# One chunk of a recurrent mixer: two matmuls moved up beside two others, and one start flag for a PSUM tile instead of three

## The chip, the cores and the metric

The kernel runs on one core of a Trainium2 chip. The metric is the device time of one execution in microseconds; several executions are given by their median. A core has five engines with a queue of instructions each: TensorE (PE, with its weight loads shown apart as PEld), VectorE (DVE), ScalarE (ACT), GpSimd (POOL) and SyncE (SP, which issues DMAs here). Engines wait for each other by semaphores only. Matmuls write PSUM; ScalarE and VectorE copy from there to SBUF.

## The reference

One decoder layer on a sequence of 2048 tokens of width 1024: an RMS norm, one input projection, two groups of heads side by side (sliding-window attention, and RWKV-7 time mixing), an output projection, a gated MLP with a short convolution, and a last norm. The change lies in the time mixing. For each of its 8 heads (64 wide) a state S of 64 x 64 is carried along the sequence:

```
def step(S, inp):
    r_t, w_t, k_t, v_t, a_t, b_t = inp
    sa = jnp.einsum('bhvk,bhk->bhv', S, a_t)
    S = S * w_t[:, :, None, :] + sa[..., None] * b_t[:, :, None, :] \
        + v_t[..., None] * k_t[:, :, None, :]
    return S, jnp.einsum('bhvk,bhk->bhv', S, r_t)
```

## The kernel before, in words

The time mixing is done in chunks of 64 tokens. The sequence has 4 blocks of 512 tokens, the 8 heads are 4 pairs, and 16 times (4 blocks x 4 pairs, here called head pairs) a chain of 8 chunks is run by `chain`, in order: 128 chunks in all. Two heads of a pair lie on partitions 0 to 63 and 64 to 127, so each product of a chunk is two instructions, one for each half (`hs`).

A chunk works on one PSUM tile `pc` with three columns of 64 and has these steps:

- W (line 896): the products with the incoming state SV, into `pc[:, 0]`, with 128 rows of the array and 64 columns for each head. ScalarE copies them to Pt.
- y1: the first half of the output, W (its other columns) with SV, into another PSUM tile, `pY`.
- TT (line 909): the inverted triangle with Pt, into `pc[:, 1]`, with 64 rows and 64 columns. ScalarE copies it to Ut.
- IK (line 913): the identity and the keys with SV, into `pc[:, 2]`: the carried state and the part of the values. It has 128 rows and 64 columns, and it does not need Ut.
- Bt (line 914): the part that comes by Ut, added in `pc[:, 2]`, with 64 rows and 64 columns. ScalarE scales the sum into the next chunk's SV.
- XB: the second half of the output, with Ut, into `pY`, with 64 rows and 64 columns.

The first `start=True` that reaches a PSUM bank clears the marks by which a later matmul knows whether to add or to overwrite.

The order of all engines in this part is written out: every matmul, activation and vector operation goes through a helper that ties it behind the one before on its engine (`in_order`; matmuls are recorded as line 104, activations as 110, vector operations as 124, GpSimd's as 132, DMAs as 170). Between the steps of a chunk `fill` places other work: the next pair's input projections (`pin_...`), its preparation, the attention, the output of the pair before. How much goes into each gap is set by tables of assumed costs, which the change leaves alone. Only DMAs and some GpSimd work are ordered by a scheduler.

For the pair that comes next one triangle per chunk has to be inverted: `px` (TensorE), `XB` (VectorE), a DMA to `dL` and back as `LL`, a substitution of 31 steps on VectorE (`Mt` and `M`, woven between its other work), a DMA to `dT` and back as `TT`, a transpose `T` on VectorE, and two small rounds of matmuls `ph`. All of it stands inside the current pair's chain.

Of the kernel before, what the change touches and what calls it, by code (L numbers as in the profile page):

```python
# [83 lines left out]
def hybrid_trunk_kernel(  # L84
# [9 lines left out]
    def in_order(key, i):  # L94
        if order["on"]:
            last = order.get(key)
            if last is not None:
                tc.add_manual_dep(i.ins, last.name,
                                  mybir.DependencyInfo(mybir.DependencyClass.NoSync, mybir.DependencyReason.DATA),
                                  reason="issue order")  # L100
            order[key] = i.ins

    def mm(**kw):
        in_order("pe", nc.tensor.matmul(**kw))  # L104
# [4 lines left out]
    def act(*args, **kw):  # L109
        in_order("act", nc.scalar.activation(*args, **kw))  # L110
# [86 lines left out]
    with ExitStack() as A:  # L197
# [20 lines left out]
        def fin512(name):  # L218
            return tp.tile([P, BLK], F32, tag="f", name=name, bufs=2)
# [76 lines left out]
        hs = [slice(0, 64), slice(64, 128)]  # L296
# [101 lines left out]
        def defer(us, fn, key=None):  # L398
            clk["n"] += 1
            todo.append((clk["t"] + us, clk["n"], fn, key))  # L400
            todo.sort(key=lambda d: d[:2])
# [6 lines left out]
        def need(key):  # L408
            while any(d[3] == key for d in todo):
                todo.pop(0)[2]()  # L410
# [213 lines left out]
        def v3(ap):  # L624
            return ap.rearrange("p (c t) -> p c t", t=C)
# [257 lines left out]
        def chain(n, fill):  # L883
            b, j = divmod(n, NPAIR)
            u = f"{b}_{j}"
            S = U[n]
            W, SV, XB, Bt, IK, TT, E = S["W"], S["SV"], S["XB"], S["Bt"], S["IK"], S["TT"], S["E"]
            St = state[j]
            pY = None
            for c in range(NCH):  # L890
                pc = ps_ch.tile([P, 3, C], F32, tag="ch", name=f"pc_{u}_{c}")
                Pt = tp.tile([P, C], F32, tag="Pt", name=f"Pt_{u}_{c}")
                Ut = tp.tile([P, C], F32, tag="Ut", name=f"Ut_{u}_{c}")
                eC = E[:, c, C:C + 1]
                for hh, s in enumerate(hs):
                    mm(out=pc[s, 0], lhsT=W[:, c, hh, 0:C], rhs=SV[:, c, hh, :], start=True, stop=True)
                act(Pt, pc[:, 0], AF.Copy)
                def y1(c=c, pY=pY):
                    for hh, s in enumerate(hs):
                        mm(out=pY[s, c], lhsT=W[:, c, hh, C:2 * C], rhs=SV[:, c, hh, :], start=True, stop=False)  # L900
                if c > 0:
                    y1()
                fill()
                if c == 0:
                    need("ycopy")
                    pY = ps_ch.tile([P, NCH, C], F32, tag="cy", name=f"pY_{u}")
                    y1(pY=pY)
                for hh, s in enumerate(hs):
                    mm(out=pc[s, 1], lhsT=TT[s, c, :], rhs=Pt[s], start=True, stop=True)
                act(Ut, pc[:, 1], AF.Copy)  # L910
                fill()
                for hh, s in enumerate(hs):
                    mm(out=pc[s, 2], lhsT=IK[:, c, hh, :], rhs=SV[:, c, hh, :], start=True, stop=False)
                    mm(out=pc[s, 2], lhsT=Bt[s, c, :], rhs=Ut[s], start=False, stop=True)
                if c < NCH - 1:
                    for hh, s in enumerate(hs):
                        act(SV[s, c + 1, hh, :], pc[s, 2], AF.Copy, scale=eC[s])
                else:
                    act(St, pc[:, 2], AF.Copy, scale=eC)
                for hh, s in enumerate(hs):  # L920
                    mm(out=pY[s, c], lhsT=XB[s, c, C:2 * C], rhs=Ut[s], start=False, stop=True)
                fill()
            Y = S["Y"] = tp.tile([P, NCH, C], F32, tag="Y", name=f"Y_{u}")
            ysq = fin512(f"ysq_{u}")

            def go0():
                act(Y, pY, AF.Copy)
                act(ysq, pY.rearrange("p c v -> p (c v)"), AF.Square, scale=0.125)
                defer(Q["y1"], go1, f"y_{u}")
            var = tp.tile([P, 8], F32, tag="var", name=f"var_{u}")  # L930

            def go1():
                vred(out=var, in_=v3(ysq), axis=AX.X, op=ALU.add)
                gts(out=var, in0=var, scalar1=LNX_EPS, scalar2=None, op0=ALU.add)
                gtt(out=var, in0=var, in1=mhalf, op=ALU.pow)
                defer(Q["y2"], go2, f"y_{u}")

            def go2():
                gtt(out=Y, in0=Y, in1=var.unsqueeze(2).broadcast_to([P, NCH, C]), op=ALU.mult)
            defer(0.1, go0, "ycopy")  # L940
# [155 lines left out]
        for n in range(-2, NU + 1):  # L1096
# [120 lines left out]
            def fill():  # L1217
                st["hop"] += 1
                was = st["done"]
                tick(Q["hop"])  # L1220
                run_until(MS + (1 - MS) * st["hop"] / hops)
                while dense and st["done"] - was < MINQ:
                    c, fn = dense.pop(0)
                    tick(c)
                    fn()
                    st["done"] += c
# [3 lines left out]
            if 0 <= n < NU:  # L1230
                chain(n, fill)
# [601 lines left out]
```

## Time and profile before

| what | value |
|---|---|
| time, median of 3 runs | 2750.26 us (2749.35 to 2753.12) |
| the profiled execution's own time | 2754.07 us |
| its span, first to last instruction | 2752.3 us |
| TensorE busy in the span | 2640.4 us, 96% |
| VectorE, ScalarE, GpSimd busy | 62%, 47%, 53% |
| mean granted clock of TensorE | 0.977 of 2.4 GHz |
| stage of the chunk chains | 126 to 1270 us |

The profile is of one execution. Durations below are in microseconds unless marked ns. A row of the order of time gives start, duration, engine, line, operation, what is written and read, and in brackets the engine's idle time before it and what ended it. An fp32 matmul instruction shows as two records. Ends of matmuls are modelled, so it is starts that are compared.

### The profile page before, as it was taken

How to read it: one execution, taken by the hardware profiler on the slowest of the kernel's cores; microseconds unless marked ns; L12 is line 12 of the kernel's file. 1: busy time of each engine (PE TensorE's matmuls, PEld its weight loads, DVE VectorE, ACT ScalarE, POOL GpSimd, SP SyncE). 2: the span in 40 equal slices, each digit the busy share in tenths (PEclk: the TensorE clock that was granted, in tenths of full speed). 3: DMA queues.
4: the chain of work that ended last, by engine and by line, in shares of the span. 5: the costliest groups of instructions: out<-in, count | busy, mean ns of one | idle time of the engine just before them, and what ended most of it. 6: DMA issues, size and time to landing. Idle time of an engine off the chain costs nothing.

```text
span 2752.3 us, 42156 instructions
## 1 busy us (share of the span) xinstructions
PE 2640.4 (96%) x15211; PEld 2051.3 (75%) x15211; DVE 1713.7 (62%) x3217; ACT 1288.9 (47%) x2737; POOL 1460.6 (53%) x1356
## 2 busy tenths in 40 slices
PE   7799999999999999998989999999999999999997
PEld 5566777777777767676867878788788888878885
DVE  6567666676667556743666677677766765453334
ACT  4356655656556545543434344336333343343343
POOL 6333443344343333422346777777666665484594
PEclk9899999999999999999999999999999999999998
DMA  4222222222223222234663444446333336743354
GB/s 128 63 61 71 70 72 69 67 55 72 64 72 95 56 61 64 75 101 135 199 213 104 151 132 142 139 164 199 107 104 111 102 98 229 245 141 100 107 173 149
DMA packets 333108, 313.94 MB, mean 114 GB/s; under 512 B 102576, under 2 KB 254274, under 8 KB 332898
## 3 DMA queue, kind: packets, MB, share of 16 engines
q1 hardware_dynamic: 332290, 310.71, 36.9%
q8 instruction: 119, 1.95, 0.3%
q14 instruction: 91, 0.75, 0.1%
q10 hardware_dynamic: 608, 0.53, 0.1%
HBM read 229.26 MB, written 81.92 MB: 113 GB/s over the span
## 4 chain that ended last, share of the span: by engine, by line
PE 74%; DVE 9%; DMA 6%; POOL 4%; issue 3%; ACT 3%; SPq 0%; POOLq 0%; ACTq 0%; DVEq 0%
PE d L104 14%; PE q_g L104 12%; PE q_u L104 12%; PE pc L104 6%; PE pin_r L104 3%; PE pin_k L104 3%; PE poa L104 3%; PE pin_q L104 3%; DVE M L124 2%; PE px L104 2%; DVE Mt L124 2%; PE pS L104 2%; PE po L104 2%; PE pO L104 1%; PE pin_v L104 1%
## 5 line engine op out<-in xcount | busy, mean ns | idle before, releaser
L1255 POOL TENSOR_TENSOR ul_a<-sa,uh_a 128x512 fp32r<-128x512 f32 x154 | 208.8, 1362 | 154.7 <-ACT uh_a L110 151.3
L1255 POOL TENSOR_TENSOR ul_u<-s_u,uh_u 128x512 fp32r<-128x512 f32 x154 | 215.7, 1410 | 137.6 <-ACT uh_u L110 131.2
L1255 POOL TENSOR_TENSOR ul_g<-s_g,uh_g 128x512 fp32r<-128x512 f32 x154 | 221.7, 1448 | 55.4 <-ACT uh_g L110 51.3
L104 PE MATMUL q_g<-h2h,uh_g 128*128 128x512 f32 x616 | 242.2, 393 | 7.8 <-DVE u_g L1470 6.3
L104 PE MATMUL q_u<-h2h,uh_u 128*128 128x512 f32 x616 | 240.2, 390 | 2.2 <-DVE ct L1470 1.5
L104 PE MATMUL q_g<-h2h,ul_g 128*128 128x512 f32 x616 | 240.7, 391 | 0.4 <-POOL ul_g L1255 0.4
L104 PE MATMUL q_g<-h2l,uh_g 128*128 128x512 f32 x616 | 241.0, 391 | 0.0
L104 PE MATMUL q_u<-h2h,ul_u 128*128 128x512 f32 x616 | 239.9, 390 | 1.0 <-POOL ul_u L1255 1.0
L104 PE MATMUL q_u<-h2l,uh_u 128*128 128x512 f32 x616 | 239.7, 389 | 0.0
L104 PE MATMUL d<-ul_b,uh_a 128*128 128x512 f32 x616 | 232.3, 391 | 6.7 <-DVE ul_b L1467 6.7
L104 PE MATMUL d<-uh_b,ul_a 128*128 128x512 f32 x616 | 227.7, 391 | 3.5 <-POOL ul_a L1255 3.5
L110 ACT ACTIVATE uh_a<-sa 128x512 fp32r<-128x512 f32 x154 | 97.3, 632 | 233.4 <-PE d L104 126.1
L104 PE MATMUL d<-uh_b,uh_a 128*128 128x512 f32 x616 | 204.1, 389 | 0.0
L110 ACT ACTIVATE uh_u<-s_u 128x512 fp32r<-128x512 f32 x154 | 94.9, 628 | 220.9 <-DVE s_u L1467 116.6
L1467 DVE TENSOR_TENSOR ul_b<-wd,uh_b 128x512 fp32r<-128x512 f32 x55 | 68.2, 1240 | 189.3 <-ACT uh_b L110 184.0
L110 ACT ACTIVATE uh_g<-s_g 128x512 fp32r<-128x512 f32 x154 | 95.1, 629 | 183.2 <-PE q_u L104 101.7
L124 DVE TENSOR_TENSOR Mt<-M,LL 128x60 f32<-128x60 f32 (+24 forms) x496 | 153.2, 309 | 35.7 <-DMA LL<-dL 27.2
L124 DVE TENSOR_TENSOR M<-M,Mt 128x60 f32<-128x60 f32 (+24 forms) x496 | 163.0, 329 | 10.9
L124 DVE SCALAR_TENSOR_TENSOR cc<-g,fcst,cc 128x1024 f32<-128x1024 f32 x88 | 145.7, 1674 | 29.1 <-ACT cc L110 28.4
L104 PEld LDWEIGHTS q_g<-h2h,uh_g 128*128 128x128 f32 x616 | 116.6, 189 | 34.7 <-DVE u_g L1470 8.0
L104 PEld LDWEIGHTS d<-ul_b,uh_a 128*128 128x128 f32 x616 | 116.3, 189 | 31.3 <-DVE ul_b L1467 7.1
L104 PEld LDWEIGHTS d<-uh_b,ul_a 128*128 128x128 f32 x616 | 115.8, 189 | 29.4 <-POOL ul_a L1255 5.6
(370 smaller groups left out, 7141.3 us busy)
## 6 DMA issues: line engine op xcount, KB each, us to landing
sa<-actc SPq DMA_DIRECT2D x77, 512.0 KB
s_g<-in_ffn_w_gate_dram SPq DMA_DIRECT2D x44, 512.0 KB
s_u<-in_ffn_w_up_dram SPq DMA_DIRECT2D x44, 512.0 KB
actc<-cc SPq DMA_DIRECT2D x88, 256.0 KB
actc<-sa SPq DMA_DIRECT2D x66, 256.0 KB
wd<-in_ffn_w_down_dram SPq DMA_DIRECT2D x22, 512.0 KB
s_cat<-catT SPq DMA_DIRECT2D x20, 512.0 KB
x<-in_x_dram SPq DMA_DIRECT2D x16, 512.0 KB
```

What stands on the lines that cost most here:

```text
L104: in_order("pe", nc.tensor.matmul(**kw))
L110: in_order("act", nc.scalar.activation(*args, **kw))
L124: in_order("dve", f(*args, **kw))
L1255: nc.gpsimd.tensor_tensor(out=out, in0=in0, in1=in1, op=ALU.subtract)
L1467: nc.vector.tensor_tensor(out=out, in0=in0, in1=in1, op=ALU.subtract)
```

## The change

The IK products are issued right behind the W products. Their `start=True`, and that of the TT products, become `start=False`: the W products' `start=True` clears the marks for all three columns of `pc`, and each column's first write overwrites.

```
                 for hh, s in enumerate(hs):
                     mm(out=pc[s, 0], lhsT=W[:, c, hh, 0:C], rhs=SV[:, c, hh, :], start=True, stop=True)
+                for hh, s in enumerate(hs):
+                    mm(out=pc[s, 2], lhsT=IK[:, c, hh, :], rhs=SV[:, c, hh, :], start=False, stop=True, skip_group_check=True)
                 act(Pt, pc[:, 0], AF.Copy)
...
                 for hh, s in enumerate(hs):
-                    mm(out=pc[s, 1], lhsT=TT[s, c, :], rhs=Pt[s], start=True, stop=True)
+                    mm(out=pc[s, 1], lhsT=TT[s, c, :], rhs=Pt[s], start=False, stop=True, skip_group_check=True)
                 act(Ut, pc[:, 1], AF.Copy)
                 fill()
                 for hh, s in enumerate(hs):
-                    mm(out=pc[s, 2], lhsT=IK[:, c, hh, :], rhs=SV[:, c, hh, :], start=True, stop=False)
-                    mm(out=pc[s, 2], lhsT=Bt[s, c, :], rhs=Ut[s], start=False, stop=True)
+                    mm(out=pc[s, 2], lhsT=Bt[s, c, :], rhs=Ut[s], start=False, stop=True, skip_group_check=True)
```

On TensorE before, the end of the second chunk of the first head pair (`pc_0_1` is that chunk's tile, `pY` the output's; `x2` are the two halves):

```order
L104 MATMUL pc_0_1_1211<-SV_0_631,IK_135 64x64
L104 MATMUL pc_0_1_1211<-Ut_0_1_1213,Bt_0_630 64x64
L104 MATMUL pc_0_1_1211<-SV_0_631,IK_135 64x64
L104 MATMUL pc_0_1_1211<-Ut_0_1_1213,Bt_0_630 64x64
L104 MATMUL pY_0_1150<-Ut_0_1_1213,XB_0_629 64x64 x2
```

Here IK and Bt alternate. In the changed kernel TensorE has in the same chunk, at its start (first three rows) and at its end (last two):

```order
L104 MATMUL pc_0_1_1211<-SV_0_631,W_0_628 64x64 x2
L104 MATMUL pc_0_1_1211<-SV_0_631,IK_135 64x64 x2
L104 MATMUL pY_0_1152<-SV_0_631,W_0_628 64x64 x2
...
L104 MATMUL pc_0_1_1211<-Ut_0_1_1213,Bt_0_630 64x64 x2
L104 MATMUL pY_0_1152<-Ut_0_1_1213,XB_0_629 64x64 x2
```

The two IK instructions stand behind W and ahead of y1 (`pY` with W), and the two Bt instructions stand together. All else on TensorE keeps its order, and so do VectorE and ScalarE in this stage.

On SyncE, the DMAs around `dL` of the third pair before (`w_q` is a weight of the input projection):

```order
L170 DMA catT<-oT_0_1314 64x512 x2
L170 DMA dL_2_2042<-XB_2_1926 32x8x32 x3
L170 DMA w_q_0_1983<-in_w_in_dram 128x8x64 x2
L170 DMA dL_2_2042<-XB_2_1926 32x8x32
L170 DMA LL_2_2047<-dL_2_2042 128x1x1024
L170 DMA w_q_0_2146<-in_w_in_dram 128x8x64 x2
```

A weight load stands inside the four writes. In the changed kernel:

```order
L170 DMA catT<-oT_0_1316 64x512 x2
L170 DMA dL_2_2044<-XB_2_1926 32x8x32 x4
L170 DMA w_q_0_1985<-in_w_in_dram 128x8x64 x2
L170 DMA LL_2_2049<-dL_2_2044 128x1x1024
L170 DMA w_q_0_2148<-in_w_in_dram 128x8x64 x2
```

The weight load that stood between the third and the fourth write of `dL` stands behind the fourth. This is so in five of the pairs. On GpSimd the copies of `state` to `SV` move forward by a few places.

## Rows read from the trace of the kernel before

**Rows 1.** Busy time by stage: PE, PEld, DVE, ACT, POOL, then clock, DMA.

```profile
126.00:1270.00 1144.00, 1121.15 (x8543) 813.69 (x8543) 744.34 (x2116) 648.34 (x1694) 446.03 (x513) 0.98 0.27 71
```

**Rows 2.** Instructions on tile pc: records, ns min/median/max, first and last start.

```profile
L104 PE MATMUL pc<-SV,IK x512: 222/270/367, 133.2 to 1266.8; 128*64 128x64 f32 x171
L104 PE MATMUL pc<-Ut,Bt x512: 218/267/366, 133.5 to 1267.0; 64*64 64x64 f32 x171
```

**Rows 3.** TensorE in order of time, one chunk.

```profile
600.25 0.34 PE L104 MATMUL pc<-SV,W 128*64 128x64 f32 x4
600.42 0.29 PE L104 MATMUL pY<-SV,W 128*64 128x64 f32 x4
600.63 0.50 PE L104 MATMUL pin_r<-hh,wh_r 128*128 128x512 f32 x1
...
602.23 0.33 PE L104 MATMUL pc<-Pt,TT 64*64 64x64 f32 x4
602.49 0.65 PE L107 MATMUL pT<-ident,P 128*128 128x128 f32 x4
...
606.38 0.33 PE L104 MATMUL pc<-SV,IK 128*64 128x64 f32 x2
606.64 0.32 PE L104 MATMUL pc<-Ut,Bt 64*64 64x64 f32 x2
606.89 0.33 PE L104 MATMUL pc<-SV,IK 128*64 128x64 f32 x2
607.15 0.27 PE L104 MATMUL pc<-Ut,Bt 64*64 64x64 f32 x1
...
607.52 1.02 PE L104 MATMUL pss<-kk,onesb 128*2 128x512 f32 x2
```

**Rows 4.** Chain of waits, fourth head pair (342 to 414): shares, pieces.

```profile
by line: DVE M L124 10.5%; PE pc L104 10.4%; PE pin_r L104 8.8%; PE pin_k L104 8.8%; DVE Mt L124 8.2%; DMA dT<-M 6.6%; PE px L104 5.8%; PE pS L104 4.6%; PE pin_av L104 4.4%; PE ph L104 2.9%; DVE P L124 2.8%; PE pO L104 2.5%; DMA TT<-dT 2.5%
...
377.15 0.91 PE pg L104 x3
...
406.40 1.09 PE ph L104 x32
```

**Rows 5.** Chain of waits, pairs 1 and 16: the IK and Bt groups.

```profile
133.27 0.97 PE pc L104 x7
...
1266.17 1.04 PE pc L104 x7
```

**Rows 6.** VectorE's waits, 126 to 1270: us in total, times, longest.

```profile
DVE T L124 <- DMA TT<-dT: 17.6, 10, 3.4
...
DVE Mt L124 <- DMA LL<-dL: 15.6, 7, 5.2
```

**Rows 7.** VectorE in order of time, fifth pair, ahead of T.

```profile
477.50 0.69 DVE L124 TENSOR_TENSOR ptl<-pT,pth 128x512 fp32r<-128x512 f32 x1 [1.85 <-ACT pth L110]
```

**Rows 8.** SyncE's DMA issues in order of time, fourth and fifth pair.

```profile
353.25 0.58 SPq L170 DMA_DIRECT2D dL<-XB  x1
356.86 0.58 SPq L170 DMA_DIRECT2D LL<-dL  x1
...
425.55 0.80 SPq L170 DMA_DIRECT2D dL<-XB  x2
427.74 0.58 SPq L170 DMA_DIRECT2D LL<-dL  x1
```

**Rows 9.** TensorE's waits, 126 to 1270: us in total, times, longest.

```profile
PE pc L104 <- ACT Pt L110: 5.0, 10, 0.8
PE ph L104 <- DVE T L124: 4.5, 7, 1.9
```

**Rows 10.** TensorE in order of time, after two idle stretches.

```profile
560.94 0.48 PE L104 MATMUL pY<-SV,W 128*64 128x64 f32 x4 [1.01 <-ACT ysq L110]
...
701.26 0.90 PE L104 MATMUL ph<-T,XB 32*32 32x32 f32 x26 [1.88 <-DVE T L124]
```

**Rows 11.** Busy time by stage, the stretch after the first of them.

```profile
560.70:574.30 13.60, 13.36 (x60) 10.24 (x62) 4.71 (x8) 4.69 (x11) 8.02 (x9) 0.50 0.14 26
```

More of the change, by code (lines that the diff above doesn't have):

```diff
@@ L896, in chain @@
                     mm(out=pc[s, 0], lhsT=W[:, c, hh, 0:C], rhs=SV[:, c, hh, :], start=True, stop=True)
+                for hh, s in enumerate(hs):
+                    mm(out=pc[s, 2], lhsT=IK[:, c, hh, :], rhs=SV[:, c, hh, :], start=False, stop=True, skip_group_check=True)
                 act(Pt, pc[:, 0], AF.Copy)
@@ L908, in chain @@
                 for hh, s in enumerate(hs):
-                    mm(out=pc[s, 1], lhsT=TT[s, c, :], rhs=Pt[s], start=True, stop=True)
+                    mm(out=pc[s, 1], lhsT=TT[s, c, :], rhs=Pt[s], start=False, stop=True, skip_group_check=True)
                 act(Ut, pc[:, 1], AF.Copy)
@@ L912, in chain @@
                 for hh, s in enumerate(hs):
-                    mm(out=pc[s, 2], lhsT=IK[:, c, hh, :], rhs=SV[:, c, hh, :], start=True, stop=False)
-                    mm(out=pc[s, 2], lhsT=Bt[s, c, :], rhs=Ut[s], start=False, stop=True)
+                    mm(out=pc[s, 2], lhsT=Bt[s, c, :], rhs=Ut[s], start=False, stop=True, skip_group_check=True)
                 if c < NCH - 1:
```

## The prediction

> **What bounds the kernel now.** I read the table by stage first, because the change touches one stage only: the chunk chain runs from 126 to 1270 us. There TensorE is busy 1121 of 1144 us at a granted clock of 0.98, VectorE 744 and ScalarE 648 [rows 1]. So a microsecond taken from TensorE's queue can be worth a microsecond of time. It is not sure to be, since TensorE's busy share says nothing of how far behind it the others are. Next I read TensorE's rows of one chunk in order of time, for what its matmuls cost in the order they stand in [rows 2, 3]. Then I read the chain of waits of each head pair's stretch, to see in how many chunks these matmuls lie on the path [rows 4, 5], and last what else waits there [rows 6 to 9].
>
> **What the chunk costs.** Every product here is two instructions, one for each half of the partitions, and every fp32 instruction is two records. IK and Bt have 512 records each, so there are 128 chunks [rows 2]. What the rows show: as long as neighbours use the same part of the array (128x64, or 64x64), the two halves run side by side. The four records of the W product begin at 600.25 and the next product, of the same shape, begins at 600.42, so they take 0.17 us. The two products together, 8 records, take 0.38 us until the first 128x128 matmul at 600.63 [rows 3]. When the shape alternates nothing runs side by side: IK, Bt, IK, Bt begin at 606.38, 606.64, 606.89 and 607.15, 0.26 us for each single instruction. The last Bt overlaps the XB product that follows it in its own shape, and all six instructions end with the next matmul's start at 607.52. That is 1.14 us [rows 3].
>
> **The change, part by part.**
> The order written into the kernel moves the two IK instructions of each chunk up behind the two W instructions. No instruction goes and none is added. After it TensorE has W, W, IK, IK, all 128x64, then later TT, TT, and then Bt, Bt, XB, XB, all 64x64.
> 1. IK's new place. It adds one more pair in an unbroken run of one shape. The bounds from the rows are 0.02 us (two halves that overlap fully, as the last Bt does with the XB product behind it) and 0.26 us (as now, alone). I take 0.12: W and its neighbour need 0.38 together and a lone pair with its change of shape 0.26 (TT, from 602.23 to 602.49), so the second pair costs the difference [rows 3].
> 2. What remains of the old place is two pairs of one shape, as W and its neighbour, 0.38 us.
> 3. So 1.14 becomes 0.12 + 0.38 = 0.50, and a chunk's TensorE time falls by 0.64 us. With the bounds of step 1 it falls by 0.50 to 0.74. Times 128 chunks that is 82 us (64 to 95).
> 4. The start flags that go (on TT and on the IK product): the Bt product is already written without one, beside IK with one, and lasts 267 against 270 ns [rows 2]. I price the flag at nothing; between these two rows the most it could be is 0.003 x 512 = 1.5 us either way.
> 5. An added wait: ScalarE's copy to Pt was released by the second W and is now released by the second IK, so it starts 0.12 us later (0.02 to 0.26). Behind it on ScalarE stand only copies that wait for TensorE too, and TensorE itself has a fill of projection matmuls before it needs Pt. In the chunk shown W is over by 600.42 and TensorE asks for Pt at 602.23 [rows 3]. It really waited for Pt ten times, 5.0 us in all [rows 9]. If each of these and as many near ones grow by 0.12, it costs 2.4 us; without any cover it would be 128 x 0.12 = 15 us.
> 6. Further down, the Bt products no longer have an IK in front of each, so the copies to SV, and the next chunk, come earlier. That shortens the chain itself and needs no price of its own.
> 7. On SyncE's queue one thing moves: in five head pairs a weight load stood between the third and fourth dL writes; now it stands behind the fourth. With it in between, LL left 3.6 us after the last dL (353.25 to 356.86). Where the writes are adjacent it left 2.2 us after the row's first (425.55 to 427.74) [rows 8]. So LL may leave 1 to 2 us earlier in those five. On GpSimd the copies state to SV move a few places forward, with nothing behind them that waits.
>
> **How much of 82 us arrives.** I followed the chain of waits for each of the 16 head pairs and counted the groups of IK and Bt that lie on it. The counts are 3, 6, 8, 5, 8, 6, 8, 5, 8, 6, 8, 5, 4, 8, 8 and 8, together 104 of 128, the first and last of them in [rows 5]. In the others the path leaves TensorE. In the fourth pair's stretch it is TensorE up to pg at 377.15, then VectorE's substitution (M and Mt, 18.7% of that stretch) then DMA and T, and TensorE again with ph at 406.40 [rows 4]. A shorter TensorE does nothing for those 29 us. First bound: 104 x 0.64 = 67 us.
>
> The second limit is the loop px, XB, dL, LL, substitution, TT, T, ph. In it only about one chunk before XB and one after ph is TensorE's; the rest is DMA and VectorE, which already wait for LL and for TT by 15.6 and 17.6 us in all [rows 6]. In the pairs that have 8 groups on TensorE's path the gain is 8 x 0.64 = 5.1 us each only if that loop has as much room. In the fifth and ninth pair's stretch T stands in VectorE's queue behind ptl, whose wait of 1.85 us is the main room [rows 7]; with the one chunk of TensorE's own and the smaller waits I allow 3.4 us each there, so 2 x 1.7 = 3.4 us are lost. That leaves 64. From it I take 2.4 for Pt (step 5) and 6.8 for the clock: TensorE will stand idle more often, as in front of ph at 701.26, where it waited 1.88 us [rows 10], and I allow one more stretch at half clock like the one of 13.6 us in the trace, which costs 13.6 x 0.5 [rows 11]. Sum: 67 - 3.4 - 2.4 - 6.8 = 54 us. From the median 2750.26 that gives 2696; the profiled execution itself, 2754.07 (span 2752.3 plus 1.8 around it), lies 3.8 above the median and would come to 2700.
>
> **Rivals.**
> A. This forecast, saving 40 to 72 us: 2678 to 2710.
> B. The loop has more room than the chain of waits shows, with the earlier LL as part of it, and nearly all 82 us arrive: 2665 to 2678. For it: TensorE waited for T only 4.5 us in all [rows 9]. Against: T was released by its DMA in ten pairs [rows 6].
> C. The loop gives back most: only chunks ahead of XB and behind ph count, 2 x 0.64 in 15 pairs plus the last pair's 5.1, which is 24 us, about 2726 (2710 to 2745). Against: VectorE's own waits on px and pS early in each stretch shrink with TensorE.
> D. The price is per instruction and not per change of shape, so that 8 instructions a chunk cost the same in any order: 2750. The overlap of W and its neighbour speaks against it [rows 3]. [...]
> E. Slower: TensorE now arrives early at ph in every pair, stops, and the clock falls for long. After a stop of 1.01 us before 560.94 the granted clock was 0.50 (1.2 GHz instead of 2.4) for 13.6 us [rows 10, 11], which costs 6.8 us. If that happened in 15 pairs, 102 us would go against 64 won, and the time would be 2788. It decides from 4.3 us lost per pair. Against: TensorE already waits for T in seven pairs, and the stage's mean clock is 0.98 [rows 1, 9]. The Trainium skill, page "TensorE: Matmul & The Clock Gate", section "HAM oscillation — how this bites in real kernels", speaks for this rival: a loop that makes TensorE wait once per turn was re-throttled in every turn. Here the trace agrees in the one place and, by the stage's mean, not as a habit.
>
> **How the numbers follow.** A 0.62, B 0.12, C 0.17, D 0.04, E 0.05. Half of C and most of B belong in the range: 2668 to 2728. Less than 0.2% (5.5 us) is what a measurement of this kernel cannot tell from no change; A, B and C lie beyond it, so faster is 0.91, same 0.04, slower 0.05.
>
> **What would show it.** In the profile after, W, IK and pY should begin within 0.3 us of each other, with Bt, Bt, XB, XB in 0.38 us (steps 1 to 3). TensorE's busy time in the chain stage should fall by about 80 us while the stage shortens less, with the difference as idle time before ph, pT or the like. Pt's copy should begin 0.12 us later after W. If the IK pair takes 0.26 us or more, or if the six instructions still need over 1 us, step 1 is wrong; if idle before ph grows by over 40 us, C is right; if the clock of the stage falls below 0.95, E.

## The result and the profile after

| | median, us | runs |
|---|---|---|
| before | 2751.69 | 2749.35 to 2756.58 (4) |
| changed | 2709.43 | 2700.87 to 2712.79 (4) |

The ratio is 0.9835, with a 95% interval from 0.9806 to 0.9864: 42 us faster, where 54 us were forecast. The time lies inside the stated range, and at the low edge of the saving that the forecast gave itself (40 to 72). The profiled execution took 2707.62 us, its span is 2705.9 us, 46.4 less than before.

One chunk of the changed kernel on TensorE, in order of time (start, duration, operation; four records are the two halves):

```profile
594.24 0.33 PE L104 MATMUL pc<-Ut,Bt 64*64 64x64 f32 x4
594.41 0.28 PE L104 MATMUL pY<-Ut,XB 64*64 64x64 f32 x4
594.62 0.39 PE L104 MATMUL pS<-kTh,q 128*128 128x256 f32 x1
...
597.46 0.34 PE L104 MATMUL pc<-SV,W 128*64 128x64 f32 x4
597.63 0.29 PE L104 MATMUL pc<-SV,IK 128*64 128x64 f32 x4
597.74 0.29 PE L104 MATMUL pY<-SV,W 128*64 128x64 f32 x4
597.96 0.66 PE L107 MATMUL pT<-ident,P 128*128 128x128 f32 x4
```

Bt and XB together now take 0.38 us (594.24 to 594.62), and the IK pair takes 0.11 (597.63 to 597.74). That is 0.49 us where [rows 3] had 1.14: 0.65 us for a chunk, 83 us for 128. The chunk shown is typical: in 124 of the 128 chunks before, all at full clock, the old group took 1.143 to 1.145 us.

The chunk stage as a whole (busy time of PE, PEld, DVE, ACT, POOL, then TensorE's granted clock, DMA share), to be read against [rows 1]:

```profile
124.00:1223.00 1099.00, 1051.61 (x8553) 763.51 (x8552) 754.95 (x2117) 645.51 (x1696) 448.08 (x514) 0.97 0.28 74
```

The stage is 45 us shorter (1144 to 1099), TensorE's busy time 70 us (1121.2 to 1051.6), and its idle time in the stage doubled, from 23 to 47 us. So 83 us of work left TensorE, and of them 25 came back as idle time. Busy time fell by 70 and not by 83; of these 13 us the lower clock explains some 9 (below), and the other 4 are not assigned. Who ends TensorE's waits now, with us in total, times and longest:

```profile
PE pT L107 <- DVE P L124: 19.9, 18, 2.4
PE pc L104 <- ACT Pt L110: 6.9, 10, 1.5
PE pc L104 <- ACT SV L110: 4.9, 7, 1.2
PE pc L104 <- ACT Ut L110: 4.1, 5, 1.1
PE pY L104 <- ACT ysq L110: 3.6, 4, 0.9
PE ph L104 <- DVE T L124: 3.5, 3, 1.7
```

And the same list before, the lines that stand beside those of [rows 9]:

```profile
PE pT L107 <- DVE P L124: 4.4, 4, 1.3
PE pY L104 <- ACT ysq L110: 4.1, 4, 1.0
PE pc L104 <- ACT Ut L110: 2.1, 4, 0.6
...
PE pc L104 <- ACT SV L110: 0.6, 1, 0.6
```

The new idle time is at pT, the transposes of the attention weights P, which VectorE normalises while it is busy with the substitution (4.4 to 19.9 us). At ph, where I had looked for it first, the wait even fell (4.5 to 3.5). Part of it also comes through ScalarE, which works in the order written. Here ScalarE, in order of time, waits 2.28 us for VectorE's m and only then gets to Ut, for which TensorE has stood idle for 1.13 us:

```profile
600.53 0.20 ACT L110 ACTIVATE m<-m 128x2 f32<-128x2 f32 x1 [2.28 <-DVE m L124]
600.64 0.49 ACT L110 ACTIVATE P<-P,m 128x256 f32<-128x256 f32 x1
...
602.72 0.22 ACT L110 ACTIVATE Ut<-pc 128x64 f32<-128x64 f32 x1
```

```profile
603.00 0.33 PE L104 MATMUL pc<-Ut,Bt 64*64 64x64 f32 x4 [1.13 <-ACT Ut L110]
```

The chain of waits of the whole stage, by line, after and before:

```profile
by line: DVE M L124 9.2%; DVE Mt L124 8.7%; PE pin_q L104 6.2%; issue 5.2%; PE poa L104 5.0%; PE pc L104 5.0%; PE px L104 4.7%; PE pin_k L104 4.4%; DMA LL<-dL 4.4%; DVE P L124 4.2%; PE pS L104 3.0%; PE ph L104 2.7%; PE pO L104 2.5%; PE pin_
```

```profile
by line: PE pc L104 13.6%; PE pin_r L104 6.8%; PE pin_k L104 6.8%; PE pin_q L104 6.5%; PE poa L104 5.2%; PE pS L104 4.9%; DVE M L124 4.6%; PE px L104 4.5%; DVE Mt L124 4.1%; PE pO L104 3.6%; PE pin_v L104 3.2%; PE ph L104 2.7%; PE pY L104 2
```

TensorE's pc fell from 13.6% to 5.0% of the path, and VectorE's substitution, M and Mt, rose from 8.7% to 17.9%. The path has moved to VectorE.

### The profile page after: what moved, and what is told of

Its sections match the earlier page's. It is cut to its first block, busy times and chain, and to the rows that moved or that the text cites. A ratio compares the mean times of both kernels' runs of the same rounds, so it can differ in the third digit from the quotient of the medians.

```text
span 2705.9 us, 42161 instructions
## 1 busy us (share of the span) xinstructions
PE 2568.1 (95%) x15211; PEld 1998.0 (74%) x15211; DVE 1722.6 (64%) x3217; ACT 1284.7 (47%) x2737; POOL 1461.2 (54%) x1356
## 4 chain that ended last, share of the span: by engine, by line
PE 63%; DVE 17%; DMA 6%; POOL 5%; issue 5%; ACT 4%; SPq 0%; POOLq 0%; ACTq 0%; DVEq 0%
PE d L104 14%; PE q_g L104 14%; PE q_u L104 12%; DVE M L124 4%; DVE Mt L124 4%; PE poa L104 3%; PE pin_q L104 2%; DMA LL<-dL 2%; PE px L104 2%; PE pc L104 2%; PE pin_k L104 2%; DVE P L124 2%; PE po L104 2%; PE ph L104 1%; PE pS L104 1%
## 5 line engine op out<-in xcount | busy, mean ns | idle before, releaser
L124 DVE TENSOR_TENSOR Mt<-M,LL 128x60 f32<-128x60 f32 (+24 forms) x496 | 159.8, 322 | 36.8 <-DMA LL<-dL 28.3
```

Source lines behind the costliest of these rows:

```text
L124: in_order("dve", f(*args, **kw))
```

## Experiments

Theory 1: a change of shape between neighbouring matmuls is what cost 0.26 us an instruction, and VectorE's loop is what kept half of the gain. The rivals are named with each run. All ratios are to the kernel before, run on the same chip.

**Grouped at the old place.**

```
-                    mm(out=pc[s, 2], lhsT=IK[:, c, hh, :], rhs=SV[:, c, hh, :], start=True, stop=False)
-                    mm(out=pc[s, 2], lhsT=Bt[s, c, :], rhs=Ut[s], start=False, stop=True)
+                    mm(out=pc[s, 2], lhsT=IK[:, c, hh, :], rhs=SV[:, c, hh, :], start=True, stop=False)
+                for hh, s in enumerate(hs):
+                    mm(out=pc[s, 2], lhsT=Bt[s, c, :], rhs=Ut[s], start=False, stop=True)
```

> Kernel before, with the two IK products standing together and then the two Bt products, at the old place (behind Ut), flags as before. Theory 1 (the price is the change of shape between neighbours): IK, IK, Bt, Bt, XB, XB has one change inside instead of three, so the group takes 0.26 + 0.38 = 0.64 us instead of 1.14, 0.50 x 128 = 64 us less TensorE time; with the same share arriving as in the changed kernel (42 of 82, about a half) the time is about 2718 us (2708 to 2728). Rival 2 (what helped is that IK left the path between Ut and SV, not that equal shapes stand together): grouping alone gives nothing, 2745 to 2755 us.

2715.3 us, ratio 0.9854 (0.9821 to 0.9887). TensorE in order of time:

```profile
598.98 0.34 PE L104 MATMUL pc<-SV,IK 128*64 128x64 f32 x4
599.24 0.33 PE L104 MATMUL pc<-Ut,Bt 64*64 64x64 f32 x4
599.41 0.28 PE L104 MATMUL pY<-Ut,XB 64*64 64x64 f32 x4
599.62 0.38 PE L104 MATMUL pS<-kTh,q 128*128 128x256 f32 x1
```

The group takes 0.64 us (598.98 to 599.62), as expected, and 36 of the 42 us are there without IK being moved at all (the two intervals overlap, so the 6 us between them are not shown). So the shapes' order is the cause, and the second rival falls. The Trainium skill says so too, page "TensorEngine Tiling (Array Packing)", section "Key Properties": a change of tiling mode drains the engine, while different tiles of one mode run side by side. The rows agree, with 0.26 us an instruction where modes alternate and 0.17 for a pair where they don't.

One more rival has no run of its own: in the old order Bt adds at once into the place that IK has just written, and the grouping ends that too. The rows speak against it. The first half's Bt (606.64 in [rows 3]) and the second half's IK (606.89) write different halves, and still start 0.25 us apart. And products of one shape that add into one place, such as these of the attention in the changed kernel (float32r, one record each), start 0.06 us apart:

```profile
603.49 0.22 PE L104 MATMUL pO<-ptl,vth 128*64 128x128 f32 x1
603.55 0.22 PE L104 MATMUL pO<-pth,vtl 128*64 128x128 f32 x1
603.61 0.22 PE L104 MATMUL pO<-pth,vth 128*64 128x128 f32 x1
```

**Only the flags.** The old order, with the new flags:

```
-                    mm(out=pc[s, 1], lhsT=TT[s, c, :], rhs=Pt[s], start=True, stop=True)
+                    mm(out=pc[s, 1], lhsT=TT[s, c, :], rhs=Pt[s], start=False, stop=True, skip_group_check=True)
...
-                    mm(out=pc[s, 2], lhsT=IK[:, c, hh, :], rhs=SV[:, c, hh, :], start=True, stop=False)
+                    mm(out=pc[s, 2], lhsT=IK[:, c, hh, :], rhs=SV[:, c, hh, :], start=False, stop=False, skip_group_check=True)
-                    mm(out=pc[s, 2], lhsT=Bt[s, c, :], rhs=Ut[s], start=False, stop=True)
+                    mm(out=pc[s, 2], lhsT=Bt[s, c, :], rhs=Ut[s], start=False, stop=True, skip_group_check=True)
```

> Kernel before in its old order, with only the flags changed: TT and IK without the clearing of marks. Theory 1 prices the flag at nothing: 2751 us, within 5. A rival by which writes without a clearing flag are cheaper or dearer: off by more than 10 us, with TT's and IK's records longer or shorter than 267 and 270 ns.

2749.6 us, ratio 0.9994 (0.9977 to 1.0011): no difference that can be measured. TT's and IK's records still last 267 and 270 ns in the median. So one clearing for all three columns has no price that can be measured.

**Half of the substitution left out, in the changed kernel and in the one before.** This and the next pair ask the same thing twice: is it VectorE's loop that kept the rest?

```
-                    woven.extend((mul, add))
+                    if i < 15:
+                        woven.extend((mul, add))
```

> Changed kernel with the last 16 of the 31 substitution steps left out (32 fewer VectorE instructions per head pair, the inverse is then incomplete). Theory 1 (what was not won of 82 us is the loop through VectorE's substitution): TensorE's waits for P, T, SV and Ut shrink from some 46 us in the stage to some 20, the clock falls less often, and the time goes from 2709 to about 2680 us (2672 to 2690). Rival 3 (the rest went to Pt's later release and to the clock alone): it stays within 2700 to 2712.

> Kernel before with the same 16 steps left out. Theory 1: TensorE is nearly the only bound there, so little is won: 2743 us (2736 to 2750), and the distance between this and the changed kernel with the same cut grows from 42 to about 63 us. Rival 3: the distance stays at 42.

Changed: 2659.3 us, ratio 0.9663 (0.9640 to 0.9685). Before: 2730.0 us, ratio 0.9930 (0.9904 to 0.9956). Both gains were larger than I expected, 50 and 21 us instead of 29 and 8. The distance between the kernels grew from 42 to 71 us. The stage rows, changed and then before, both with the cut:

```profile
115.00:1177.00 1062.00, 1038.80 (x8546) 755.91 (x8545) 616.56 (x1636) 646.46 (x1694) 448.87 (x513) 0.98 0.29 76
```

```profile
118.00:1246.00 1128.00, 1117.32 (x8544) 812.88 (x8544) 607.65 (x1636) 648.96 (x1695) 447.15 (x513) 0.98 0.27 72
```

TensorE's busy time now differs by 78.5 us, near the 83 that were taken from it, and the stage by 66. Its idle time is 23 us in the changed kernel (47 without the cut) and 11 in the one before (23). The wait at pT, 19.9 us in the changed kernel, is down to 7.9 with the cut:

```profile
PE pT L107 <- DVE P L124: 7.9, 6, 2.2
```

(The 46 us in the expectation for the changed kernel are all of TensorE's waits in the stage; P, T, SV and Ut are 32 of them.) With a shorter substitution most of TensorE's gain arrives. The third rival, Pt and the clock alone, falls: it had the distance stay at 42. The cut shortens VectorE's work as a whole and the chain of the substitution with it, and so does the edit of the next pair; which of the two counts is not told apart.

**The weight split on VectorE during the substitution.** Most of VectorE's 992 instructions M and Mt take some 0.2 us. In the trace of the changed kernel 107 take over 0.7 us, most of them about 1.2, and each of these began while GpSimd was in an instruction of its own. Here are VectorE and GpSimd over the same 5 us:

```profile
380.71 1.27 DVE L124 TENSOR_TENSOR M<-M,Mt 128x28 f32<-128x28 f32 x1
381.90 0.19 DVE L124 RECIPROCAL nq<-nq 128x8 f32<-128x8 f32 x1
382.02 1.21 DVE L124 TENSOR_TENSOR Mt<-M,LL 128x24 f32<-128x24 f32 x1
...
383.49 0.99 DVE L124 TENSOR_TENSOR M<-M,Mt 128x24 f32<-128x24 f32 x1
...
384.74 0.16 DVE L124 TENSOR_TENSOR Mt<-M,LL 128x16 f32<-128x16 f32 x1
```

```profile
380.66 1.28 POOL L132 TENSOR_TENSOR BK<-BK,sw 128x512 f32<-128x512 f32 x1 [6.23 <-DVE BK L124]
381.90 2.54 POOL L132 TENSOR_TENSOR wl_av<-w_av,wh_av 128x512 fp32r<-128x512 f32 x2
```

The longer M (128x28) lasts 1.27 us beside a GpSimd instruction of 1.28 us that began 0.05 us earlier. It ends 0.04 us behind that one (381.98 and 381.94), and the M of 383.49 ends as closely behind the second of GpSimd's two subtractions (384.48 and 384.44). The edit gives such a subtraction to VectorE itself, where it costs 0.7 us, and issues it 0.9 us (of the written order's own clock) behind the copy it needs:

```
-            gtt(out=wl[:, ks], in0=w32[:, ks], in1=f32(wh[:, ks]), op=ALU.subtract)
...
-                w_dma()
+            late = bool(woven)
+
+            def low():
+                (tt if late else gtt)(out=wl[:, ks], in0=w32[:, ks], in1=f32(wh[:, ks]), op=ALU.subtract)
+                if half == 1:
+                    w_dma()
+            if late:
+                defer(0.9, low, f"ws_{name}")
+            else:
+                low()
...
+                        need(f"ws_{nm}")
```

> Changed kernel; while a substitution is under way, the subtraction that splits an input weight (wl, 128x512) is done by VectorE (0.69 us by the row of ptl) instead of GpSimd. In the changed kernel 107 of the 992 instructions of the substitution last about 1.2 us instead of 0.2, and some 78 of them lie beside such a subtraction on GpSimd. Theory 1 with the addition that GpSimd's subtraction holds VectorE up: VectorE's loop gets 0.3 us shorter for each, the long M and Mt rows fall below 40, and the time goes to about 2697 us (2685 to 2709). Rival: the long rows come from elsewhere, or VectorE now waits for the ScalarE copy in front of each subtraction, and the time rises, 2712 to 2735.

> Kernel before (IK and Bt alternating) with the weight split on VectorE during the substitution, as in the run that took the changed kernel to 2670. Theory 1: before the change TensorE's own work sets most of the stage and VectorE's loop only part of it, so the same edit is worth less here: about half of the 39 us, 2730 us (2722 to 2740), and the distance between the two kernels with this edit is about 60 us instead of 42. Rival: the edit helps by itself, whatever TensorE does, and gives 39 us here too: 2705 to 2718.

In the changed kernel it gives 2670.1 us, ratio 0.9704 (0.9678 to 0.9731), 39 us on top of the change and more than the 12 I expected (the intervals of the two ratios lie apart). In the kernel before it gives 2738.7 us, ratio 0.9948 (0.9927 to 0.9970), 14 us and less than the half I expected. The distance between the kernels is 69 us, so the second, independent way of relieving VectorE gives the same answer as the first. The long rows fell from 107 to 59, not below 40: of the 78 rows that I had counted beside a subtraction only 62 began inside one, and 18 of those are left. The substitution's groups in the stage (count, busy us, mean ns), changed kernel and then with the split:

```profile
L124 DVE TENSOR_TENSOR M<-M,Mt 128x60 f32<-128x60 f32 (+24 forms) x465 | 153.7, 331 | 10.0
L124 DVE TENSOR_TENSOR Mt<-M,LL 128x60 f32<-128x60 f32 (+24 forms) x465 | 148.8, 320 | 24.3 <-DMA LL<-dL 16.6
```

```profile
L124 DVE TENSOR_TENSOR M<-M,Mt 128x60 f32<-128x60 f32 (+24 forms) x465 | 127.2, 273 | 9.4
L124 DVE TENSOR_TENSOR Mt<-M,LL 128x60 f32<-128x60 f32 (+24 forms) x465 | 127.1, 273 | 23.0 <-DMA LL<-dL 16.1
```

VectorE's M and Mt got 48 us shorter. TensorE's idle time in the stage is 26 us with the split, and its wait at pT 11.3. GpSimd has less to do as well (393 us busy in the stage instead of 448), and what that alone is worth was not tried. The stage row and the wait, with the split:

```profile
124.00:1186.00 1062.00, 1035.94 (x8543) 753.47 (x8543) 726.90 (x2163) 646.02 (x1694) 392.83 (x466) 0.98 0.28 76
```

```profile
PE pT L107 <- DVE P L124: 11.3, 11, 2.3
```

**The same grouping in the attention scores**, and with the split.

```
-                           start=True, stop=False)
+                           start=e == 0, stop=False, skip_group_check=True)
+                    for e in range(2):
...
-                           start=False, stop=True)
+                           start=False, stop=True, skip_group_check=True)
```

> Changed kernel; in the attention scores the same two ideas: the two 128-row products (with kTh) of a group stand together, then the two 64-row products (with kTl), with one clearing of marks for the bank. Now each of the four takes 0.31 us because the shapes alternate. Theory 1: the second of each pair costs about 0.12 us, 0.38 us less per group, 64 groups, 24 us less TensorE time; as TensorE waits for VectorE in half of the stage about a half arrives: 2697 us (2688 to 2705). Rival: a change between 128 and 64 rows is not what costs there, and the time stays within 2705 to 2713.

> Changed kernel with both edits, the weight split on VectorE during the substitution and the grouped scores. Theory 1: with the loop through VectorE shorter more of TensorE's gain arrives, 2682 us (2668 to 2697), more than the sum of the two alone. Rival: what the two give alone does not add, 2695 or more.

Grouped scores alone: 2692.0 us, ratio 0.9787 (0.9751 to 0.9824), 17 us more than the change gives by the medians, though the two intervals overlap, so this gain is likely and not shown. TensorE's row of one group:

```profile
586.03 0.50 PE L104 MATMUL pS<-kTh,q 128*128 128x256 f32 x2
586.46 0.50 PE L104 MATMUL pS<-kTl,q 64*128 64x256 f32 x2
586.89 0.50 PE L104 MATMUL pin_gd<-hh,wh_gd 128*128 128x512 f32 x1
```

Two like products take 0.43 us; a group of four takes 0.86, where the changed kernel's four rows of 0.31 (594.62 and on) make 1.25. With both edits it was 2676.5 us, ratio 0.9726 (0.9690 to 0.9762), no better than the split alone. The two edits do not add. In that profile TensorE waits 21.6 us for P, as in the changed kernel, and its mean clock over the span is 0.972, against 0.979 with the split alone.

**More products on VectorE.** To the split, first:

```
-                gtt(out=BK[:, :, 1], in0=v3(S["kp"]), in1=v3(S["En"]), op=ALU.mult)
+                (tt if woven else gtt)(out=BK[:, :, 1], in0=v3(S["kp"]), in1=v3(S["En"]), op=ALU.mult)
```

The second run has `order.get("sub")` in the place of `woven`, there and in the split, a mark set where the substitution is written and cleared behind it. The third adds the grouped scores.

> Changed kernel with the weight split on VectorE during the substitution, and of the products into BK (128x512, GpSimd, 1.28 us, beside 32 of the long rows) those that fall into a substitution on VectorE too. If GpSimd's long instructions hold up VectorE's short ones for about 1 us each and cost 0.7 us there, the long rows fall from 59 to about 30 and the time to about 2662 us (2654 to 2670). Rival: VectorE now waits for their inputs from GpSimd and ScalarE, and the time rises to 2672 or more.

> As the run with the weight split on VectorE, but the choice is made by a mark set from the start of a substitution to its end in the written order (not by whether steps are still to be woven in, by which the run before moved none of the products into BK), and it covers the weight split and the products into BK. 59 long rows are left with the split alone, 32 beside weight splits and 22 beside BK products. If GpSimd's long instructions hold VectorE up, the long rows fall to about 35 and the time from 2670 to about 2660 us (2652 to 2668). Rival: TensorE's own work is the bound again (its idle time in the stage is down to 26 us), or VectorE pays 0.7 us where it saves 1.0, and nothing moves: 2667 to 2676.

> The same with the grouped scores, 25 us less TensorE time. Theory 1: VectorE's loop is still the tighter one, so TensorE's gain arrives by less than half: 2655 us (2645 to 2665). Rival: with the loop relieved all of it arrives, 2640 or less; or nothing does, as in the run with both edits: 2668 to 2680.

The first, 2668.8 us, ratio 0.9705 (0.9667 to 0.9743), tells nothing new: the condition never held where the BK products are written down, so the order was that of the split alone (which it repeats within 1.3 us). With a mark set from the start of the substitution to its end, 7 of the 32 BK products and four more splits (55 for 51) went to VectorE: 2662.9 us, ratio 0.9664 (0.9630 to 0.9697), long rows from 59 to 44. The interval overlaps that of the split alone, so the step is not shown. With the grouped scores as well it is 2657.9 us, ratio 0.9642 (0.9612 to 0.9672): the lowest median of a version with the whole computation, 98 us below the kernel before on the same chip (2756.18) and 51 below the change's own median. That it beats the change is shown (the intervals of the two ratios lie apart). That the last two edits add to the split is not: the interval lies just below that of the split (0.9678 to 0.9731) but overlaps that of the first run of this group (0.9667 to 0.9743), which has the same order.

## Why the prediction came out as it did

- Steps 1 to 3, TensorE's price: right. IK's pair took 0.11 us (0.12 expected), Bt and XB 0.38, a chunk 0.49 (0.50), 83 us in all (82).
- Step 4, the flags: right, shown by the run with the flags alone.
- Step 5, Pt: right in size, and that by luck. Where Pt's copy waited for TensorE it starts 0.12 us later behind W (0.56 us for 0.44 in the median), as said, and TensorE's waits for Pt rose from 5.0 to 6.9 us; 2.4 were allowed. But they rose nearly as much in the run grouped at the old place, where Pt's release is as before:

```profile
PE pc L104 <- ACT Pt L110: 6.5, 10, 1.3
```

With the split on VectorE they are 2.6 us in the changed kernel and 2.9 in the one before. So the later release cost nothing that these runs show, and the rise goes with VectorE's loop.

- Step 7, LL: right about when it leaves. In the fourth pair LL now leaves at 343.92, 1.3 us after the weight load behind the last dL; SyncE's rows:

```profile
341.42 1.08 SPq L170 DMA_DIRECT2D dL<-XB  x2
342.60 0.40 SPq L170 DMA_DIRECT2D w_ak<-in_w_in_dram  x1
343.92 0.58 SPq L170 DMA_DIRECT2D LL<-dL  x1
```

The last dL, the second of the first row, leaves at 341.77, so LL follows it by 2.2 us where [rows 8] has 3.6. In the five pairs it was 3.1 to 3.6 us and is now 1.8 to 2.6. That it helped is not shown: VectorE's wait for LL is 16.6 us in the stage, 15.6 before.

- How much arrives: right that the loop through VectorE keeps the rest, and by about how much. I had taken 15 us for chunks off the path (82 - 67), 3.4 for the loop's room and 2.4 for Pt, 21 us together; idle time grew by 25. The place was wrong in part: the sum has TensorE wait in front of ph, and only the signs name pT beside it. The waits came at pT, and through ScalarE's queue at SV and Ut, so that the size fits so well is partly luck. The loop holds TensorE back at each result of VectorE that falls inside the substitution, not only at its end.
- The clock cost more than "one more stretch at half clock", 6.8 us. By the clock records of the two traces TensorE was granted 1.2 GHz in place of 2.4 for 41 us of the stage before and for 59 after, which is 9 us of full clock more. The longest such stretch after:

```profile
541.60:558.50 16.90, 16.60 (x76) 13.14 (x77) 4.88 (x8) 6.01 (x13) 8.02 (x9) 0.50 0.26 57
```

It began in a stop of 0.90 us in front of the row pY at 541.90, the same place as that of [rows 10, 11] in the kernel before. Over the span the mean went from 0.977 to 0.973. The changed kernel's four executions took 2700.9 us at 0.977, 2707.6 at 0.973, 2711.2 at 0.972 and 2712.8 at 0.971: the two go together, and at the clock of before it would have saved some 50 us, an estimate from one execution. That more short stops cause the lower clock fits these runs, but was not tried by itself; the run with the flags alone, in the old order, had 0.975 in its profile, so some of it is chance.
- The sum, by the two profiles: 83 us left TensorE, 25 came back as idle time, 9 by the clock and 4 are not assigned, which leaves the stage's 45. The forecast had 82, 21 and 6.8. So no single term was far out; idle time and clock were each put somewhat too low. The medians differ by 42, 4 less than the two profiled spans.
- Of the rivals, the time is A's, at its edge: about half arrived. C's sign, idle time in front of ph up by over 40 us, did not come: ph's fell, and all of it together grew by 25. B needed room in the loop that was not there, and in the two runs that made room the kernels lie 71 and 69 us apart. D is refuted by the grouping at the old place: the same instructions take 0.64 us instead of 1.14. E did not come: the stage's clock is 0.97.

## What to carry to other kernels

Look at the shapes of neighbouring small matmuls, not only at their number: alternating 128-row and 64-row products cost 0.26 us each here, and the same products side by side in equal shapes half or less. Where such a move leaves two groups of products open at once in a PSUM tile, one clearing of the marks can serve both, as here; it cost nothing that could be measured. Before counting such a gain, follow the chain of waits through each stretch and count how often these matmuls lie on it; what lies on it otherwise is the next thing to shorten. The change and the split together gave 80 us (2750.35 to 2670.07), where the change alone gave 42 and the split alone 14.

## What the runs showed of the hardware that I had not expected

In this kernel GpSimd's long instructions held up VectorE's short M and Mt until they ended. M of 128x28 elements took 1.27 us beside a GpSimd product of 1.28 us, and 0.19 elsewhere in the same substitution:

```profile
356.78 0.19 DVE L124 TENSOR_TENSOR M<-M,Mt 128x28 f32<-128x28 f32 x1
```

In the whole trace of the changed kernel, 840 of the 992 instructions M and Mt began with no GpSimd instruction under way, and none of these took over 0.24 us. 112 began while GpSimd was in a TENSOR_TENSOR, and every one of them ended 0.02 to 0.15 us behind it, up to 1.35 us long. The Trainium skill, page "GPSIMD Engine Reference", section "Specifications", says that its SBUF interfaces are shared with VectorE and names VectorE's instructions with two SBUF inputs as a case of contention; M and Mt are such, and the rows agree. The rows also show it for P's normalisation, for which TensorE waits at pT: 107 of its 128 instructions began with GpSimd free and took 0.36 us at most, and 13 of the others took 1.06 to 1.46. It was dearer to have GpSimd do a 1.28 us subtraction beside the substitution than to let VectorE do it in 0.7 us: moving 51 of them took 39 us off the changed kernel, and 14 off the kernel before.
